# Rotary partners 64 partitions apart, two exchange transfers a half tile; gate and memory stores issued by ScalarE

## The chip, the core and the metric

The kernel runs on one core of a Trainium2 chip. The metric is the device time of one execution in microseconds (us). Five engines work in parallel, each through its own list in a fixed order: PE (matmul, with its weight loads shown as PEld), DVE (VectorE), ACT (ScalarE), POOL (GpSimd) and SP (SyncE, which here only issues transfers). 16 DMA engines carry the transfers. They synchronise through semaphores, so an instruction that waits holds everything behind it on its own engine.

## The reference

One layer of a hybrid encoder over 1024 tokens of width 1024: a mixer (windowed attention beside a gated delta rule), cross-attention into 256 memory tokens, a feed-forward block. What the change touches is the rotary embedding of attention queries and keys, the gate of the delta rule's output, and the memory's keys and values:

```python
def _rope(x, positions):                      # x: (b, s, heads, 64)
    half = x.shape[-1] // 2
    ...
    x1, x2 = xf[..., :half], xf[..., half:]
    return jnp.concatenate([x1 * cos - x2 * sin, x2 * cos + x1 * sin], axis=-1)
...
proj = h @ w_in[l]
aq, ak, av, dqkv, dgate, dalpha, dbeta = jnp.split(proj, IN_SPLITS, axis=-1)
aq = _rope(aq.reshape(b, s, ATTN_HEADS, ATTN_HEAD_DIM), positions)
ak = _rope(ak.reshape(b, s, ATTN_KV_HEADS, ATTN_HEAD_DIM), positions)
...
o = o * jax.nn.silu(gate.astype(jnp.float32).reshape(b, s, DN_HEADS, DN_HEAD_V))
...
kv = mem_n @ w_kv
k = kv[..., :D_MODEL].reshape(b, m, CROSS_HEADS, CROSS_HEAD_DIM)
v = kv[..., D_MODEL:].reshape(b, m, CROSS_HEADS, CROSS_HEAD_DIM)
```

Within a head of 64 values, value i and value i + 32 are rotary partners: each of the two outputs needs both.

## The kernel before

**Layout.** Activations of the mixer lie turned: features on the 128 partitions, tokens along the free axis in two halves of 512. Matmuls of float32 data run in three passes: each operand is split into a rounded part and a rest (`split`, L100: an ACT cast, then a DVE or POOL subtraction, L103 and L104), and hi x hi, lo x hi and hi x lo are summed in PSUM (`gemm_b`, L257). `load_w` (L118) fetches a weight tile of 128 input rows x 8 x 128 columns and splits it; `proj` (L265) multiplies it with the turned input, giving two PSUM tiles of 128 features x 512 tokens.

**Stages.** First the input is normalised and the delta rule's q, k, v are projected, convolved and turned into products (`ORDER_1`). Second come, in the order of `ORDER_2`, the attention projections (A: `attn_proj`, four tiles of queries and one of keys, tile 4), the attention values (V), the gates (G: `gate_proj`, four tiles), the last levels of the delta rule's block inverses (L: `levels`, which loads blocks of the base inverse, `d_inv`, and stores its result to `d_pz`), and the first attention windows (W). Third comes the scan over eight chunks in both directions for two groups of heads (`scan`, loads of `kv` and `pz`), and between its steps the other windows and the memory's keys (K) and values (V) (`ORDER_3`). Then follow output projection, cross-attention and feed-forward, from L1053 on.

**Rotary.** In `attn_proj` (L750) a half tile of 128 features (two heads of 64) x 512 tokens is multiplied by the sines into `sn` (L757) and by the cosines into `rop` (L758). Partners are 32 partitions apart, so the sine product has to change partitions: four transfers from SBUF to SBUF, each of 32 partitions, copy `sn` into `rot` with neighbouring groups of 32 exchanged (L760 to L762). The sum (L763) is stored as 128 rows of 512 values to `d_q` or `d_k` in DRAM (L764). The sign of the sine comes from a constant column (L72). `sn` and `rot` are two halves of one tile with two buffers; `rop` has two buffers, which it shares with the gate tile `gt`. Windows load queries back from `d_q` (`qr`, L644) and keys from `d_k` (`kraw`, L700), with the features of a head in their natural order.

**Stores.** Every transfer of the program is issued by SP, in one list: the gate stores (L784), the stores of memory keys (L953) and of memory values (L971) too. The gate store waits for the Silu of ACT (L783), the other two for the ACT copy out of PSUM (L952, L970). `d_gate` is read in the second half of the scan, `d_mk` and `d_mv` before cross-attention (L1127).

**Order.** The program is written as above, but a scheduler that works from a timeline model sets the order of each engine's list when it is built; weight loads have a higher priority (`AHEAD`). An edit in one place therefore moves instructions nearby.

Of the kernel before, what the change touches and what calls it, by code (L numbers as in the profile page):

```python
# [19 lines left out]
P = 128  # L20
S = 1024
D = 1024
KT = D // P
NT = S // P
HALF = 512
# [18 lines left out]
_ROPE_AT = len(_NAMES) * P  # L44
# [3 lines left out]
def host_constants():  # L48
    i = np.arange(P)
    blk = i // 32  # L50
    a, b = i[:, None], i[None, :]
    ba, bb = blk[:, None], blk[None, :]
    tri = {
        "ident": a == b,
        "mU": a < b,
        "mL": a > b,
        "mUi": a <= b,
        "mLi": a >= b,
        "m5": (ba // 2 == bb // 2) & (ba != bb),
        "m6": ba // 2 != bb // 2,  # L60
        "ones": a + b >= 0,
    }
    out = np.zeros((P, _NCONST), np.float32)
    for n, m in tri.items():
        out[:, _AT[n]:_AT[n] + P] = m

    out[:, _AT["band0"]:_AT["band0"] + P] = np.where(b >= a, 0.0, NEG)
    out[:, _AT["band2"]:_AT["band2"] + P] = np.where(b <= a, 0.0, NEG)
    half = np.arange(32, dtype=np.float32)
    inv = np.power(np.float32(10000.0), -half / np.float32(32)).astype(np.float32)  # L70
    out[:, _ROPE_AT] = inv[i % 32]
    out[:, _ROPE_AT + 1] = np.where(i % 64 < 32, 1.0, -1.0)  # L72
    return out


# [1 line left out]
def tile_hybrid_block(  # L77
# [4 lines left out]
    g_ffn_pre, w_gate_up, w_down, g_ffn_post, consts, out, dump=None, stop=None,  # L82
):
    nc = tc.nc
    x, mem, out = x[0], mem[0], out[0]
    w_in, w_out, w_cq, w_ckv, w_co = w_in[0], w_out[0], w_cq[0], w_ckv[0], w_co[0]
# [7 lines left out]
    def f32(ap):  # L94
        return ap.bitcast(F32)
# [4 lines left out]
    def split(hi, lo, src, scale=None, eng=None):  # L100

        if scale is None:
            nc.scalar.copy(hi, src)  # L103
            return (eng or nc.vector).tensor_tensor(lo, src, f32(hi), ALU.subtract)  # L104
        nc.scalar.activation(hi, src, AF.Identity, scale=scale)
        return nc.vector.scalar_tensor_tensor(lo, src, scale, f32(hi), ALU.mult, ALU.subtract)

    def pool(name, bufs, **kw):
        return tc.tile_pool(name=name, bufs=bufs, reuse_waits="tile", **kw)
# [5 lines left out]
    dram = ctx.enter_context(tc.tile_pool(name="dram", bufs=1, space=DRAM))  # L115
    wp = ctx.enter_context(pool("wp", 2))

    def load_w(src, k, n, eng=None, after=None, place=None):  # L118

        with tc.high_priority(AHEAD):  # L120
            raw = place or wp.tile([P, k, n], F32, tag="wraw", name="wraw")
            with ExitStack() as order_:
                if after:
                    order_.enter_context(tc.issue_after(after.ins))
                nc.sync.dma_start(raw, src.rearrange("(k p) n -> p k n", p=P))
            hi = wp.tile([P, k, n], F32R, tag="whi", name="whi")
            lo = wp.tile([P, k, n], F32R, tag="wlo", name="wlo")
            split(hi, lo, raw, eng=eng)
        return hi, lo


# [44 lines left out]
    d_q = dram.tile([512, S], F32, name="d_q")  # L176
    d_k = dram.tile([P, S], F32, name="d_k")
    d_gate = dram.tile([512, S], F32, name="d_gate")
# [7 lines left out]
    d_mk = dram.tile([D, ML], F32, name="d_mk")  # L186
    d_mv = dram.tile([2, P, D], F32, name="d_mv")
# [24 lines left out]
    for hf in range(2):  # L212
        hi = hx.tile([P, KT, HALF], F32R, name=f"hhi{hf}")
        lo = hx.tile([P, KT, HALF], F32R, name=f"hlo{hf}")
        for j in range(4):
            t = 4 * hf + j
# [9 lines left out]
            for kq in range(2):  # L226
# [4 lines left out]
                o = slice(4 * kq, 4 * kq + 4), slice(j * P, (j + 1) * P)  # L231
# [25 lines left out]
    def gemm_b(whi, wlo, act, psums, nk=KT):  # L257

        for ah, p_ in zip(act, psums):
            for k in range(nk):  # L260
                for i, (w, a) in enumerate(((whi, 0), (whi, 1), (wlo, 0))):
                    nc.tensor.matmul(p_, w[:, k, :], ah[a][:, k, :], start=(k == 0 and i == 0),  # L262
                                     stop=(k == nk - 1 and i == 2))

    def proj(src_cols, eng=None):  # L265
        whi, wlo = load_w(src_cols, KT, P, eng)
        pp = [pg.tile([P, 512], F32, tag="pg", name="pg") for _ in range(2)]
        gemm_b(whi, wlo, hT, pp)
        return pp
# [23 lines left out]


    ws = [load_w(dcols(1, h), KT, P, after=xload[t]) for h, t in ((0, 1), (1, 3))]
    pps = [[None, None], [None, None]]
    for hf in range(2):
# [14 lines left out]
    for hf in range(2):  # L312
        pp = pg.tile([P, 512], F32, tag="pg", name="pg")
# [67 lines left out]
    for hf in range(2):  # L381
        sl = slice(hf * HALF, (hf + 1) * HALF)
# [363 lines left out]
    def pair():  # L746
        t = ra.tile([P, 2, HALF], F32, tag="rr", name="rr", bufs=2)
        return t[:, 0], t[:, 1]

    def attn_proj(ct):  # L750
        pp = proj(w_in[:, ct * P:(ct + 1) * P])
        dst = d_q[ct * P:(ct + 1) * P, :] if ct < 4 else d_k
        for hf in range(2):
            sl = slice(hf * HALF, (hf + 1) * HALF)
            rop = trp.tile([P, HALF], F32, tag="rop", name="rop")
            sn, rot = pair()
            nc.vector.tensor_tensor(sn, pp[hf], sinT[:, sl], ALU.mult)  # L757
            nc.vector.tensor_tensor(rop, pp[hf], cosT[:, sl], ALU.mult)  # L758

            for q in range(4):  # L760
                o = 32 * (q ^ 1)
                nc.sync.dma_start(rot[32 * q:32 * q + 32], sn[o:o + 32])  # L762
            nc.vector.tensor_tensor(rop, rop, rot, ALU.add)  # L763
            nc.sync.dma_start(dst[:, sl], rop)  # L764

    def value_proj():

# [10 lines left out]
    def gate_proj(h):  # L778

        pp = proj(w_in[:, 2304 + h * P:2304 + (h + 1) * P])  # L780
        for hf in range(2):
            gt = trp.tile([P, HALF], F32, tag="rop", name="gt")
            nc.scalar.activation(gt, pp[hf], AF.Silu)  # L783
            nc.sync.dma_start(d_gate[h * P:(h + 1) * P, hf * HALF:(hf + 1) * HALF], gt)  # L784

    issue(ORDER_2, {"A": attn_proj, "V": value_proj, "G": gate_proj, "L": levels, "W": next_windows})
    dump("d_q", d_q); dump("d_k", d_k); dump("d_gate", d_gate)
    p1.close()
# [153 lines left out]
    def next_keys():  # L942

        ct = kv_done[0]
        kv_done[0] += 1
        whi, wlo = load_w(w_ckv[:, ct * P:(ct + 1) * P], KT, P, nc.gpsimd)
        pp = pc.tile([P, 512], F32, tag="pc", name="pck")[:, 0:ML]
        for k in range(KT):
            for i, (w, a) in enumerate(((whi, 0), (whi, 1), (wlo, 0))):
                nc.tensor.matmul(pp, w[:, k, :], mT[a][:, k, :], start=(k == 0 and i == 0), stop=(k == KT - 1 and i == 2))  # L950
        cv = mk.tile([P, 512], F32, tag="cv", name="cv", bufs=2)[:, 0:ML]
        nc.scalar.copy(cv, pp)  # L952
        nc.sync.dma_start(d_mk[ct * P:(ct + 1) * P, :], cv)  # L953

    def next_values():

        ch = kv_done[1]
        kv_done[1] += 1
        pp = [pc.tile([P, 512], F32, tag="pc", name="pcv") for _ in range(2)]
        for kp in range(4):  # L960
            whi, wlo = load_w(w_ckv[kp * 256:(kp + 1) * 256, D + ch * 512:D + (ch + 1) * 512], 2, 512)
            for t in range(2):
                for kk in range(2):
                    k = 2 * kp + kk
                    for i, (w, a) in enumerate(((whi, 0), (whi, 1), (wlo, 0))):
                        nc.tensor.matmul(pp[t], mT[a][:, k, t * P:(t + 1) * P], w[:, kk, :], start=(k == 0 and i == 0),
                                         stop=(k == KT - 1 and i == 2))
        for t in range(2):
            vv = mk.tile([P, 512], F32, tag="cv", name="vv", bufs=2)
            nc.scalar.copy(vv, pp[t])  # L970
            nc.sync.dma_start(d_mv[t, :, ch * 512:(ch + 1) * 512], vv)  # L971

    scans = [scan(g) for g in range(2)]

    def scan_step(pairs):

        for _ in range(4):
            for s_ in pairs:
                next(s_, None)

    issue(ORDER_3, {"s": lambda *gs: scan_step([scans[g] for g in gs]), "W": next_windows, "M": memory_norm,
                    "K": next_keys, "V": next_values})
    dump("d_pz", d_pz[0] + d_pz[1])
    dump("d_kv", d_kv)
# [124 lines left out]
    for hf in range(2):  # L1109
        for kp in range(4):  # L1110
            k2 = slice(2 * kp, 2 * kp + 2)
            raw = raws[hf]
# [22 lines left out]
    raw = LR2.enter_context(pool("raw2", 1, side="right")).tile([P, KT, HALF], F32, name="oraw")  # L1135
# [362 lines left out]
    for e in range(EARLY):  # L1498
        f = 2 * e
        w, A = [], []  # L1500
        for i, c0 in enumerate((f * P, FF + f * P)):
            place = fw.tile([P, KT, P], F32, tag=f"fw{i}", name="wraw") if e == EARLY - 1 else None
            whi, wlo = first_gate[i] if e == 0 else load_w(w_gate_up[:, c0:c0 + P], KT, P, place=place)
# [270 lines left out]
    for t in range(4):  # L1774
# [13 lines left out]
        r = 4 + t  # L1788
# [41 lines left out]
```

## Time and profile before

| | us |
|---|---|
| median of 3 runs | 1531.19 |
| lowest and highest run | 1529.92, 1532.13 |
| the profiled execution | 1531.03 |
| its span, first to last instruction | 1529.3 |
| ScalarE (ACT) busy | 752.0 |
| GpSimd (POOL) busy | 364.1 |
| granted TensorE clock, mean share of full | 0.994 |
| first exchange transfer issued, last | 208.7, 326.2 |
| first gate store issued, last | 268.2, 365.1 |
| first store of memory keys issued, last of memory values | 394.9, 557.4 |

Times in the profile count from the start of the span. A line such as L764 is the line of the kernel printed above. SPq, PEq and the like are an engine's issuing of instructions; "x4" counts instructions; "<-" behind an idle time names what ended it. A transfer has two times: the issue on its engine, and its landing, when its data has arrived and its semaphore is complete.

### The profile page before, as it was taken

To read this page: it belongs to the slowest core of one execution; us is meant where nothing else is said; L and a number is where in the kernel's file an instruction comes from. 1 tells how busy PE (TensorE), PEld (TensorE's weight loads), DVE (VectorE), ACT (ScalarE), POOL (GpSimd) and SP (SyncE) were. 2 spreads that over 40 slices of the span, in tenths; PEclk is the share of its full clock that TensorE was granted. 3 is DMA by queue.
4 is the path that set the end of the run, shared out by engine and by line. 5 is a ranking of instruction groups with operands and counts; after the bars stand their busy time and mean duration, and the time that the engine had idled before them with its cause. 6 is when DMAs were issued, how large, how long until landed. Compare 5 with 4: busy or idle time off the path is not lost.

```text
span 1529.3 us, 21202 instructions
## 1 busy us (share of the span) xinstructions
PE 1475.7 (96%) x7403; PEld 1239.1 (81%) x7403; DVE 1116.3 (73%) x1805; ACT 752.0 (49%) x1541; POOL 364.1 (24%) x369
## 2 busy tenths in 40 slices
PE   6999999998999999999999999999999999999997
PEld 5888888877889778888788877888888888888786
DVE  6868999787888866538567768676867774696665
ACT  5578821447557764455544685223222332454532
POOL 2020221311226203252201002433534342000021
PEclk9999999999999999999999999999999999999999
DMA  6235575856987584458725554343434333853355
GB/s 208 76 109 148 144 194 142 218 176 173 322 279 236 186 296 152 141 167 271 241 97 173 192 182 134 97 138 116 146 109 153 124 103 111 321 208 97 104 177 167
DMA packets 275159, 261.06 MB, mean 171 GB/s; under 512 B 34904, under 2 KB 206829, under 8 KB 275053
## 3 DMA queue, kind: packets, MB, share of 16 engines
q1 hardware_dynamic: 275053, 259.71, 53.9%
q8 instruction: 58, 0.95, 0.3%
q14 instruction: 48, 0.39, 0.1%
HBM read 181.25 MB, written 75.79 MB: 168 GB/s over the span
## 4 chain that ended last, share of the span: by engine, by line
PE 61%; DVE 10%; DMA 10%; ACT 4%; issue 3%; SPq 2%; POOL 1%; DVEq 0%; POOLq 0%; ACTq 0%
PE pD L1481 7%; PE pE L1481 7%; PE pA L1481 6%; PE pmg L1071 6%; PE pdX L1687 6%; PE pst L1287 5%; PE pcq L262 4%; PE pB L1481 3%; PE psc L810 2%; PE pdA L1687 2%; PE pdD L1687 2%; PE pg L262 2%; DMA wraw<-in_w_gate_up_dram 1%; PE pco L1186 1%; PE pdX L1784 1%
## 5 line engine op out<-in xcount | busy, mean ns | idle before, releaser
L103 ACT CAST whi<-wraw 128x1024 fp32r<-128x1024 f32 x96 | 100.8, 1051 | 133.0 <-DMA wraw<-in_w_gate_up_dram 37.0
L262 PE MATMUL pg<-hlo,whi 128*128 128x512 f32 x352 | 139.1, 396 | 0.0
L262 PE MATMUL pg<-hhi,whi 128*128 128x512 f32 x352 | 139.1, 396 | 0.0
L262 PE MATMUL pg<-hhi,wlo 128*128 128x512 f32 x352 | 138.1, 393 | 0.0
L104 POOL TENSOR_TENSOR wlo<-wraw,whi 128x1024 fp32r<-128x1024 f32 x36 | 88.3, 2453 | 189.6 <-ACT whi L103 188.2
L1481 PE MATMUL pA<-b,whi 128*128 128x512 f32 x352 | 111.9, 400 | 3.6 <-ACT m L1508 2.8
L104 DVE TENSOR_TENSOR wlo<-wraw,whi 128x1024 fp32r<-128x1024 f32 x60 | 76.0, 1269 | 46.0 <-ACT whi L103 42.4
L1481 PEld LDWEIGHTS pA<-b,whi 128*128 128x128 f32 x352 | 66.5, 192 | 19.2 <-ACT m L1508 4.0
L1687 PE MATMUL pdX<-dhl,whi 128*128 128x512 f32 x264 | 76.1, 390 | 1.5 <-ACT dhl L103 0.8
L262 PEld LDWEIGHTS pg<-hhi,whi 128*128 128x128 f32 x352 | 66.3, 189 | 13.4 <-ACT hhi L103 0.2
L262 PEld LDWEIGHTS pg<-hhi,wlo 128*128 128x128 f32 x352 | 66.2, 188 | 12.8
L262 PEld LDWEIGHTS pg<-hlo,whi 128*128 128x128 f32 x352 | 66.2, 188 | 12.7
L1564 POOL TENSOR_TENSOR act<-act,up 128x512 f32<-128x512 f32 x33 | 50.7, 1538 | 83.1 <-DVE up L1563 61.8
L1481 PE MATMUL pA<-b,wlo 128*128 128x512 f32 x176 | 69.9, 398 | 0.5 <-DVE wlo L104 0.5
L103 ACT CAST whi<-araw 128x1024 fp32r<-128x1024 f32 (+1 forms) x36 | 35.3, 982 | 67.9 <-PE pdX L1687 27.6
L104 DVE TENSOR_TENSOR wlo<-araw,whi 128x1024 fp32r<-128x1024 f32 (+1 forms) x36 | 40.9, 1135 | 36.1 <-ACT whi L103 35.7
L1536 POOL TENSOR_TENSOR sr<-wraw 128x512 f32<-128x512 f32 x22 | 30.3, 1379 | 150.7 <-DMA wraw<-in_w_gate_up_dram 98.7
L287 DVE SCALAR_TENSOR_TENSOR acc<-cp,cols,acc 128x1024 f32<-128x1024 f32 x48 | 62.1, 1297 | 0.1
L1687 PEld LDWEIGHTS pdX<-dhl,whi 128*128 128x128 f32 x264 | 49.3, 188 | 12.7 <-ACT dhl L103 1.1
L1721 POOL TENSOR_SCALAR frs<-sq 128x1 f32<-128x1 f32 x8 | 11.9, 1497 | 194.5 <-ACT jk L1706 193.6
L103 ACT CAST dhl<-b 128x512 fp32r<-128x512 f32 x66 | 40.3, 620 | 31.6 <-PE pdA L1687 13.7
L1481 PE MATMUL pB<-s0h,s1h 128*128 128x512 f32 x176 | 54.5, 391 | 0.0
(484 smaller groups left out, 4285.5 us busy)
## 6 DMA issues: line engine op xcount, KB each, us to landing
wraw<-in_w_gate_up_dram SPq DMA_DIRECT2D x54, 512.0 KB, 3.9
kv<-d_kv SPq DMA_DIRECT2D x32, 512.0 KB, 7.5
wraw<-in_w_in_dram SPq DMA_DIRECT2D x22, 512.0 KB, 4.2
b<-in_w_down_dram SPq DMA_DIRECT2D x20, 512.0 KB, 8.0
araw<-d_as SPq DMA_DIRECT2D x20, 512.0 KB, 3.7
pz<-d_pz SPq DMA_DIRECT2D x32, 256.0 KB, 7.6
wraw<-in_w_ckv_dram SPq DMA_DIRECT2D x16, 512.0 KB, 6.3
wraw<-in_w_out_dram SPq DMA_DIRECT2D x16, 512.0 KB, 3.7
```

The source lines that it names most:

```text
L103: nc.scalar.copy(hi, src)
L104: return (eng or nc.vector).tensor_tensor(lo, src, f32(hi), ALU.subtract)
L262: nc.tensor.matmul(p_, w[:, k, :], ah[a][:, k, :], start=(k == 0 and i == 0), stop=(k == nk - 1 and i == 2))
L287: nc.vector.scalar_tensor_tensor(acc, cp[:, t:t + S], taps[t], acc, ALU.mult, ALU.add)
L810: nc.tensor.matmul(out[:, d, h, :], lt[:, d, h, :], rt[:, d, h, :], start=True, stop=True)
L1071: nc.tensor.matmul(pp[t], act[a][:, k, tt], w_[:, kk, :], start=(k == 0 and i == 0), stop=(k == KT - 1 and i == 2))
L1186: nc.tensor.matmul(po, vr_[a][:, kt, cs], pts[kt][b_], start=(kt == 0 and i == 0), stop=(kt == 1 and i == 2))
L1287: nc.tensor.matmul(bank, a[:, tt], w, start=(start and i == 0), stop=(stop and i == 2), skip_group_check=not check)
L1481: nc.tensor.matmul(out_, w[a][:, k, :], xx[b_][:, k, :], start=(start and k == 0 and i == 0), stop=(k == HK - 1 and i == 2), skip_group_ch ...
L1536: nc.gpsimd.tensor_tensor(s[0], b_[:, 0:HK], b_[:, HK:], ALU.add)
L1564: nc.gpsimd.tensor_tensor(o_, o_, up, ALU.mult)
L1687: nc.tensor.matmul(banks[t], a[:, k - k0, tt], w, start=(first and k == 0 and i == 0), stop=(k == NB - 1 and i == 2), skip_group_check=not ...
```

## The change

The weight columns of the five attention tiles are put in another order as they are split: `load_w` gets `turned_pairs`, and with it casts and subtracts in two parts, so that the first halves (32 features) of both heads stand in columns 0 to 63 and the second halves in columns 64 to 127. After the matmul, partners are then 64 partitions apart. The exchange takes two transfers of 64 partitions. The sign column changes with the layout. The store takes the features back to their natural order in DRAM, in two transfers of 64 partitions, whose destination is 2 heads x 32 features x 512 tokens. Apart from that, the stores of gates, memory keys and memory values are issued by ScalarE.

```diff
-    out[:, _ROPE_AT + 1] = np.where(i % 64 < 32, 1.0, -1.0)
+    out[:, _ROPE_AT + 1] = np.where(i < 64, 1.0, -1.0)
...
-    def load_w(src, k, n, eng=None, after=None, place=None):
+    def load_w(src, k, n, eng=None, after=None, place=None, turned_pairs=False):
...
-            split(hi, lo, raw, eng=eng)
+            if turned_pairs:
+                for a in range(2):
+                    to = [t[:, :, 64 * a:64 * a + 64].rearrange("p k (h r) -> p k h r", h=2) for t in (hi, lo)]
+                    split(*to, raw.rearrange("p k (h a r) -> p k h a r", h=2, a=2)[:, :, :, a], eng=eng)
+            else:
+                split(hi, lo, raw, eng=eng)
...
-    def proj(src_cols, eng=None):
-        whi, wlo = load_w(src_cols, KT, P, eng)
+    def proj(src_cols, eng=None, **kw):
+        whi, wlo = load_w(src_cols, KT, P, eng, **kw)
...
-        pp = proj(w_in[:, ct * P:(ct + 1) * P])
-        dst = d_q[ct * P:(ct + 1) * P, :] if ct < 4 else d_k
+        pp = proj(w_in[:, ct * P:(ct + 1) * P], turned_pairs=True)
+        dst = (d_q[ct * P:(ct + 1) * P, :] if ct < 4 else d_k).rearrange("(h a r) t -> a h r t", h=2, a=2)
...
-            for q in range(4):
-                o = 32 * (q ^ 1)
-                nc.sync.dma_start(rot[32 * q:32 * q + 32], sn[o:o + 32])
+            for a in range(2):
+                nc.sync.dma_start(rot[64 * a:64 * a + 64], sn[64 - 64 * a:128 - 64 * a])
             nc.vector.tensor_tensor(rop, rop, rot, ALU.add)
-            nc.sync.dma_start(dst[:, sl], rop)
+            for a in range(2):
+                nc.sync.dma_start(dst[a, :, :, sl], rop[64 * a:64 * a + 64])
...
-            nc.sync.dma_start(d_gate[h * P:(h + 1) * P, hf * HALF:(hf + 1) * HALF], gt)
+            nc.scalar.dma_start(d_gate[h * P:(h + 1) * P, hf * HALF:(hf + 1) * HALF], gt)
...
-        nc.sync.dma_start(d_mk[ct * P:(ct + 1) * P, :], cv)
+        nc.scalar.dma_start(d_mk[ct * P:(ct + 1) * P, :], cv)
...
-            nc.sync.dma_start(d_mv[t, :, ch * 512:(ch + 1) * 512], vv)
+            nc.scalar.dma_start(d_mv[t, :, ch * 512:(ch + 1) * 512], vv)
```

## The prediction, made before the result was known

> **What bounds the kernel now.** I read the page first, then the busy time by stage, then the chain of waits in the stage that the change touches.
>
> ```profile
> span 1529.3 us, 21202 instructions
> PE 1475.7 (96%) x7403; PEld 1239.1 (81%) x7403; DVE 1116.3 (73%) x1805; ACT 752.0 (49%) x1541; POOL 364.1 (24%) x369
> ...
> 190.00:340.00 150.00, 145.16 (x783) 122.42 (x781) 128.25 (x252) 51.03 (x124) 34.97 (x53) 1.00 0.71 188
> 340.00:380.00 40.00, 36.28 (x231) 31.66 (x229) 30.27 (x78) 29.13 (x65) 5.30 (x9) 1.00 0.55 151
> 380.00:560.00 180.00, 168.69 (x1172) 152.97 (x1173) 146.28 (x362) 114.49 (x291) 60.14 (x70) 0.97 0.83 261
> 560.00:880.00 320.00, 317.57 (x1563) 266.10 (x1561) 202.41 (x297) 169.56 (x331) 69.81 (x54) 1.00 0.55 184
> ```
>
> Columns of the stage rows: length, then PE, weight load, DVE, ACT and POOL busy (instructions), granted clock, share of the DMA engines, GB/s. The ten rotary half tiles lie between 207 and 333 us, the gate stores between 268 and 366, the memory key and value stores between 394 and 558. So the change lives in 190 to 560. PE is idle there for 370 - (145.16 + 36.28 + 168.69) = 19.9 us: that is about all that better order or earlier transfers can give (busy PE includes pipelining, so a little more may hide in it). From 560 on PE is idle 2.4 us in 320 and nothing is edited.
>
> The granted clock is full, so matmul work is fixed and the question is what its inputs wait for. The chain of waits over 185 to 380 us names it:
>
> ```profile
> by line: PE pg L262 10.3%; DMA d_pz<-Z 8.9%; DMA kv<-d_kv 6.0%; issue 5.7%; DMA rr<-rr 5.0%; DVE acc L287 4.8%; SPq L762 3.8%; DMA qr<-d_q 3.5%; DVE D L588 2.9%; SPq L565 2.0%; DMA d_inv<-A 2.0%; DVE wlo L104 1.9%; PE ps L604 1.8%; PE ps L6
> ...
> 216.91 3.08 DMA cz<-d_inv
> ...
> 226.86 4.09 DMA rr<-rr
> ...
> 331.07 7.06 DMA d_pz<-Z
> ...
> 371.87 11.68 DMA kv<-d_kv
> ```
>
> Many short links, and the largest that are not PE are landings of transfers: stores of the level matrices, the exchange, loads of the scan. PE runs in a fixed order, so a late landing stops it even where projection matmuls stand behind. A change that makes transfers land later is therefore paid, one that frees issue time gains little.
>
> **The change part by part.** The sum is made against the profiled execution, 1531.03 us (its span 1529.3 plus 1.7 around it); the median of the runs is 1531.19.
>
> *Exchange, 40 transfers to 20.*
>
> ```profile
> 237.82 2.42 SPq L762 DMA_DIRECT2D rr<-rr  x4
> 244.22 0.33 SPq L764 DMA_DIRECT2D d_q<-rop  x1
> ...
> 248.54 1.12 SPq L700 DMA_DIRECT2D kraw<-d_k  x2
> ```
>
> Four issues of 32 partitions hold SP 2.42 us; two of 64 partitions, the shape of the key loads, 1.12. That is 1.3 us a half tile, 13 over ten. The chain has SPq L762 at 3.8% of 195 us, 7.4 us; 1.12/2.42 of that remains, so at most 4.0 goes. Lower bound of the gain 0, as the last landing may be hidden anyway. PE has 4.8 us idle in 190 to 340 to give; I take half the upper bound: -2.
>
> *The stores of the rotated tiles, 10 to 20.* The transfer of 128 rows becomes two, whose destination is written 2 x 32 x 512: the leading dimension counts 2, where it counted 128. On SP it is 2 x 0.56 for 0.33, +0.8 a half tile after the add, which only takes back part of the 13 us. What matters is how many of the 16 DMA engines carry it. No transfer here has a leading dimension of 2. The nearest rows are five narrow loads at the start; the answer for the first 30 us lists 24 issues, all landed:
>
> ```profile
> DMA packets 6445, 7.59 MB, mean 253 GB/s; under 512 B 728, under 2 KB 5165, under 8 KB 6445
> ...
> rows<-in_conv_w_dram SPq DMA_DIRECT2D x1, 30.0 KB, 7.7
> rows<-in_g_cross_pre_dram SPq DMA_DIRECT2D x1, 4.0 KB
> rows<-in_g_mem_dram SPq DMA_DIRECT2D x1, 4.0 KB
> rows<-in_g_ffn_pre_dram SPq DMA_DIRECT2D x1, 4.0 KB
> rows<-in_g_dn_out_dram SPq DMA_DIRECT2D x1, 0.5 KB
> prm<-in_a_log_dram SPq DMA_DIRECT2D x1, 4.0 KB, 5.6
> ```
>
> Of the 728 small packets, 3 x 128 are the 32-byte rows of the three prm loads. 344 remain, marks of completion. 24 transfers with 16 each would leave 384; 40 are missing, and loads of 60, 8, 8, 8 and 1 rows leave 40 if they run on 15, 8, 8, 8 and 1 engines (1 + 8 + 8 + 8 + 15). So a transfer runs on as many engines as divide its leading dimension. The price comes from one store seen alone, 244.2 to 246.3 us:
>
> ```profile
> DMA packets 144, 0.26 MB, mean 125 GB/s; under 512 B 16, under 2 KB 16, under 8 KB 144
> ...
> q1 hardware_dynamic: 144, 0.26, 33.0%
> ```
>
> 33.0% of 16 engines over 2.1 us are 11.1 engine-us. On 16 engines that is 0.69 us each, on two 5.54. Lower bound of the extra: 0 (spread as now). Upper: 4.85 us a half tile on two engines, 48.5 over ten. I take the upper, since the narrow loads are nearer in shape than any 128-row store. The Trainium skill's "DMA: Bandwidth & Descriptors", section "Why a DMA increments its semaphore by 16 and not by 1", says the engine count is the largest number up to 16 that divides the slowest dimension of both sides; the 40 missing marks agree, by it this store gets two engines, and with sixteen the sum below would be 8 us lower.
>
> What is late then:
>
> ```profile
> 209.00:332.00 123.00, 119.22 (x648) 100.89 (x647) 103.22 (x215) 41.88 (x106) 32.57 (x51) 1.00 0.70 181
> ...
> L588 DVE TENSOR_TENSOR Z<-cz,dmask 128x512 f32<-128x512 f32 x16 | 11.3, 724 | 7.3 <-DMA d_pz<-Z 7.0 <-DMA cz<-d_inv 0.3
> ```
>
> Those engines are busy 0.70 x 123 = 86.1 us already; with 48.5 they need 134.6 in 123, so they end 11.6 us behind. Every 128-row transfer has a share on them and lands when the last does: the other exchange half, cz and Ul for the levels, d_pz stores (DVE already waits 7.0 us for their landing before it can rewrite Z), qr, and the first kv and pz loads. The built order puts eight such stores of A0 and A1 within two tiles, straight ahead of the level stores and the stores of the second base inverse. PE's idle 123 - 119.2 = 3.8 us absorbs part: 11.6 - 3.8 = 7.8. Bounds of the exposure 0 and, with each of cz, rr and kv late by one pair besides, 11.6 + 5.5 = 17. I take +8.
>
> *Gate and memory stores issued by ACT.*
>
> ```profile
> SPq L691 <- DVE ao L690: 12.8, 4, 3.9
> ...
> SPq L784 <- ACT z L615: 10.8, 1, 10.8
> ...
> SPq L953 <- ACT cv L952: 4.3, 2, 3.7
> ...
> L784 SPq DMA_DIRECT2D d_gate<-gt x8: 326/382/932, 268.2 to 365.1; - x8
> ...
> L953 SPq DMA_DIRECT2D d_mk<-cv x8: 320/332/811, 394.9 to 515.9; - x8
> ```
>
> SP loses a wait of 10.8 us between 336 and 348, but next behind it stands the store of ao, which has its own wait, then a d_pz store that needs the level result; the scan's loads of kv need what the last projection frees. So the relief is worth little: bounds 0 and -4 (the PE idle of 340 to 380 is 3.7), taken -1. ACT gets 20 issues of 0.33 to 0.38 us, 7 us. Behind each wait the next casts and exponentials. ACT is busy 194.7 of 370 us, which covers it at 0; uncovered it is +7. The Trainium skill, same page, section "Issuing engines are not separate DMA queues", says transfers from several engines share the same 16 and only issue time is saved; no run here shows the second queue, and by it this part stays at -1.
>
> *Split in halves.* A 128x1024 cast becomes two of 128x512, and the subtraction likewise.
>
> ```profile
> L103 ACT CAST whi<-wraw x18: 1031/1048/1057, 378.3 to 555.9; 128x1024 fp32r<-128x1024 f32 x18
> ...
> L646 ACT CAST qs<-qr x16: 617/620/643, 284.1 to 506.7; 128x512 fp32r<-128x512 f32 x16
> ...
> L757 DVE TENSOR_TENSOR rr<-pg,sct x10: 677/686/692, 207.9 to 322.2; 128x512 f32<-128x512 f32 x10
> ...
> L104 DVE TENSOR_TENSOR wlo<-wraw,whi x10: 1214/1224/1765, 499.4 to 557.0; 128x1024 fp32r<-128x1024 f32 x10
> ```
>
> ACT: 2 x 0.62 - 1.05 = 0.19, DVE: 2 x 0.69 - 1.22 = 0.16, five tiles each: 1.0 and 0.8. Both sit ahead of a projection, DVE is busy 128 of 150 us: bounds 0 and 2, taken +1.
>
> *Order.* The built program moves more than the edit: DVE issues the casts and rotary steps of A0's halves together, PE runs the two halves of a level's block side by side instead of staggered. The same matmuls, and the first scan product and the last projection stand at the same place in PE's work. Bounds -10 and +10 (half the 19.9 us of idle either way), taken 0.
>
> Sum: 1531.0 - 2 + 8 - 1 + 0 + 1 + 0 = **1537 us**.
>
> **The rivals.**
>
> *The relief of SP rules, faster.* If the stores are hidden, or spread, the exchange gives its 4.0, the gate wait its 4, and the new order part of its 10: 1531 - 8 = 1523. For it: SPq L762 is in the chain; the store is the last step of its tile, and its readers (kraw, qr) come much later. Against: the 40 missing marks.
>
> *Nothing to be seen.* Late landings eat what SP frees: 1531 within 0.2% (3 us, about what a measurement of this kernel can tell from no change). Both terms are small against 1531, but they would have to match.
>
> *ACT holds the scan.* Where transfers back up, a store's issue can hold its engine as long as SP's longest gate store, 0.93 us, instead of 0.33; between 380 and 560 ACT is busy 64% and PE waits for its casts. 20 x 0.9 = 18 us, half exposed, on top of the stores: 1537 + 9 = 1546. It decides as soon as ACT's issues average over 0.6 us.
>
> *It doesn't do what it says.* A rotary tile's issues fall from 10 to 8 only, since the stores double. If the exchange is not on the path either, what is left is +8 + 1: 1540, inside the forecast.
>
> **How the numbers follow.** Slower by the stores, around 1537: 0.55. ACT besides, around 1546: 0.12. No difference: 0.07. Faster, around 1523: 0.26. The forecast's own range is 1533 to 1548 (exposure 4 to 17 us beside small terms of a few). The faster case holds more than 2 in 10, so the range must reach it: 1522 to 1556, the top from 17 for the stores and half the loss of order or ACT. Faster by over 0.2%: 0.26, within: 0.08, slower: 0.66.
>
> **What would show it.** Stores: d_q<-rop and d_k<-rop of 128 KB landing in over 4 us (2.0 now), the kv, cz and rr landings longer, DVE's wait before Z over 7.0. If they land in 2, the term of +8 falls and the faster case is left. Exchange: 20 issues of about 0.56 us, SPq L762's successor near half of its 3.8% of the chain. Gates: no SP wait for L784 or L953, ACT's issues near 0.35. PE's idle between 190 and 380 should grow from 8.6 to some 15 us, the first output projection matmul start after 556 us, and all behind it keep its length. An earlier start of it would prove me wrong.

## The result, and the profile after

| | before | after |
|---|---|---|
| median, us | 1530.67 (5 runs, 1528.84 to 1532.13) | 1571.31 (5 runs, 1566.61 to 1573.84) |
| ratio, 95% interval | | 1.0265, 1.0245 to 1.0284 |
| span of the profiled execution, us | 1529.3 | 1568.4 |
| first scan product, first output projection matmul, us | 365.7, 555.6 | 398.1, 594.6 |

The change makes the kernel 40.6 us slower. The direction was forecast, the size was not: 1537 was said, with 1556 as the upper end.

The head of the page of after, with what the DMA queues moved:

```profile
span 1568.4 us, 21197 instructions
PE 1488.2 (95%) x7403; PEld 1252.3 (80%) x7403; DVE 1113.8 (71%) x1810; ACT 753.5 (48%) x1546; POOL 360.6 (23%) x369
...
DMA packets 274719, 261.05 MB, mean 166 GB/s; under 512 B 34464, under 2 KB 206389, under 8 KB 274613
```

The span grew by 39.1 us. PE's busy time grew by 12.5 for the same 7403 matmuls (1475.7 before), so 26.6 us are idle time of PE and 12.5 us are matmuls that took longer (the last section shows how). The packets under 512 B confirm the engine count of the stores. Before had 34904 of them:

```profile
DMA packets 275159, 261.06 MB, mean 171 GB/s; under 512 B 34904, under 2 KB 206829, under 8 KB 275053
```

By the prediction's reading each engine that carries a transfer leaves one small packet, its mark of completion. Twenty transfers fewer in the exchange take away 20 x 16 = 320 marks. Ten stores with 16 marks each are 160, twenty with 2 each are 40, which takes away 120. Together that is 440, and 34904 - 34464 = 440.

Busy time by stage, columns as in the prediction:

```profile
190.00:340.00 150.00, 134.05 (x674) 113.82 (x673) 110.11 (x219) 42.53 (x107) 30.86 (x51) 0.92 0.63 157
340.00:380.00 40.00, 34.59 (x166) 29.05 (x165) 24.25 (x58) 15.27 (x35) 1.49 (x2) 0.83 0.40 124
380.00:560.00 180.00, 162.27 (x1198) 152.30 (x1197) 141.82 (x374) 113.39 (x304) 64.89 (x77) 0.97 0.77 232
```

In 190 to 340 PE is busy 11.1 us less than before although its matmuls are slower (granted clock 0.92, it was 1.00), and the DMA engines are less busy too: 0.63 where they were 0.71. The same rows on fewer engines did not fill the engines. They left them emptier.

What DVE waits for names the place. This is the tile of the exchange in after: its issues on SP (ns shortest, median, longest), then the idle time that ended with its landing (us in total, times). Below it are the same wait and the landing times (us) in before:

```profile
L766 SPq DMA_DIRECT2D rr<-rr x20: 462/584/2234, 207.6 to 346.7; - x20
...
  DMA rr<-rr: 26.2, 7
```

```profile
  DMA rr<-rr: 1.8, 1
...
DMA to landing us min/median/max: 1.9/2.0/5.8
```

And this is the chain of waits of after over 185 to 420 us, with four of its steps (start and length in us, then what):

```profile
by line: DMA rr<-rr 17.6%; PE pg L267 10.1%; DMA pz<-d_pz 7.8%; DMA d_pz<-Z 7.6%; issue 4.1%; DVE acc L292 3.8%; DMA wraw<-in_w_ckv_dram 3.6%; PE ps L609 3.4%; DVE A L552 3.2%; DVE tmpb L550 3.1%; DVE Z L593 2.7%; DVE rr L762 2.4%; SPq L766
...
257.26 0.61 DVE rr L762
257.89 0.51 SPq L766
258.44 6.78 DMA rr<-rr
265.31 0.69 DVE rop L767
```

The exchange's landings are 17.6% of 235 us, 41 us of the chain; before they were 5.0% of 195, some 10 us. One of them took 6.78 us: the product is ready at 257.9, SP issues at once, and the add starts at 265.3. Two short stretches show what the DMA engines do meanwhile:

```profile
252.00:254.00 2.00, 2.00 (x10) 1.68 (x9) 1.96 (x5) 0.00 (x0) 0.48 (x2) 1.00 0.13 42
...
263.00:264.00 1.00, 1.00 (x10) 0.92 (x8) 0.00 (x0) 0.00 (x0) 0.00 (x0) 1.00 0.13 51
```

A share of 0.13 is 2 of 16 engines. Two engines work off the stores issued at 249.5 to 252.1 and what stands behind them, so fourteen of sixteen are idle on average, and the exchange, which has rows on all sixteen, can't land before these two have reached its rows. DVE's timeline shows the next one, and what it makes late:

```profile
276.01 0.69 DVE L767 TENSOR_TENSOR rop<-rop,rr 128x512 f32<-128x512 f32 x1 [4.52 <-DMA rr<-rr]
...
277.46 0.43 DVE L632 TENSOR_SCALAR Z<-ps 64x256 f32<-64x256 f32 x1
```

DVE stands 4.52 us at an add whose result is needed much later, and a level result, `Z`, which PE needs at once, is behind it in DVE's list. (In this wait the other engines are not idle to the end: a weight load that SP issued at 271.1, behind the exchange, brings the share to 0.76 and more from 272 to 275.)

### The profile page after: what moved, and what is told of

Its sections match the earlier page's. It is cut to its first block, busy times and chain, and to the rows that moved or that the text cites. A ratio compares the mean times of both kernels' runs of the same rounds, so it can differ in the third digit from the quotient of the medians.

```text
span 1568.4 us, 21197 instructions
## 1 busy us (share of the span) xinstructions
PE 1488.2 (95%) x7403; PEld 1252.3 (80%) x7403; DVE 1113.8 (71%) x1810; ACT 753.5 (48%) x1546; POOL 360.6 (23%) x369
## 2 busy tenths in 40 slices
DMA packets 274719, 261.05 MB, mean 166 GB/s; under 512 B 34464, under 2 KB 206389, under 8 KB 274613
## 4 chain that ended last, share of the span: by engine, by line
PE 65%; DVE 12%; DMA 11%; ACT 5%; issue 3%; POOL 1%; SPq 1%; ACTq 0%; DVEq 0%; POOLq 0%
PE pD L1486 7%; PE pE L1486 7%; PE pg L267 7%; PE pA L1486 6%; PE pmg L1076 6%; PE pdX L1692 6%; PE pst L1292 5%; PE pdA L1692 4%; PE pcq L267 3%; PE pB L1486 3%; DMA rr<-rr 3%; PE psc L815 2%; PE pdD L1692 2%; PE pdX L1789 1%; DMA wpart<-in_w_co_dram 1%
## 5 line engine op out<-in xcount | busy, mean ns | idle before, releaser
L103 ACT CAST whi<-wraw 128x1024 fp32r<-128x1024 f32 (+1 forms) x101 | 101.3, 1008 | 161.8 <-PE pg L267 39.5
L267 PE MATMUL pg<-hhi,wlo 128*128 128x512 f32 x352 | 141.3, 402 | 0.0
L104 DVE TENSOR_TENSOR wlo<-wraw,whi 128x1024 fp32r<-128x1024 f32 (+1 forms) x65 | 75.1, 1160 | 49.3 <-ACT whi L103 46.7
```

## The experiments

Each ratio is to the runs of before that were made beside it (their medians lie between 1529.1 and 1531.6). "Wide" stores run on 16 engines, "narrow" ones on 2.

| kernel | median, us | ratio | 95% interval |
|---|---|---|---|
| after (narrow, 20 stores on ACT) | 1571.3 | 1.0265 | 1.0245 to 1.0284 |
| after, those 20 stores back on SP | 1559.2 | 1.0206 | 1.0181 to 1.0231 |
| after, stores wide | 1539.8 | 1.0070 | 1.0049 to 1.0090 |
| after, stores wide and those 20 back on SP | 1530.4 | 1.0004 | 0.9994 to 1.0015 |
| after, stores wide, gate alone on ACT | 1534.0 | 1.0020 | 1.0006 to 1.0035 |
| before, 20 stores on ACT | 1539.7 | 1.0063 | 1.0042 to 1.0085 |
| before, gate stores alone on ACT | 1527.6 | 0.9992 | 0.9982 to 1.0002 |
| before, memory stores alone on ACT | 1540.3 | 1.0073 | 1.0059 to 1.0088 |
| before, memory stores on GpSimd | 1532.6 | 1.0016 | 1.0003 to 1.0029 |
| before, store written 2 x 64 x 512 (still wide) | 1529.6 | 1.0004 | 0.9988 to 1.0020 |
| before, narrow by padding | 1555.7 | 1.0176 | 1.0160 to 1.0191 |
| the same, issued by ACT | 1554.9 | 1.0165 | 1.0144 to 1.0186 |
| before, wide, issued by ACT | 1531.8 | 1.0013 | 1.0000 to 1.0026 |
| before, 4 early of 10 narrow | 1539.3 | 1.0052 | 1.0034 to 1.0070 |
| before, 4 late of 10 narrow | 1540.9 | 1.0061 | 1.0038 to 1.0083 |

### Which part of the change it is

*After, with the stores of gates and memory on SP.*

```diff
-            nc.scalar.dma_start(d_gate[h * P:(h + 1) * P, hf * HALF:(hf + 1) * HALF], gt)
+            nc.sync.dma_start(d_gate[h * P:(h + 1) * P, hf * HALF:(hf + 1) * HALF], gt)
...
-        nc.scalar.dma_start(d_mk[ct * P:(ct + 1) * P, :], cv)
+        nc.sync.dma_start(d_mk[ct * P:(ct + 1) * P, :], cv)
...
-            nc.scalar.dma_start(d_mv[t, :, ch * 512:(ch + 1) * 512], vv)
+            nc.sync.dma_start(d_mv[t, :, ch * 512:(ch + 1) * 512], vv)
```

> After, with the 20 stores of gates and of memory keys and values issued by SP again; the rotary part stays. Theory A (the stores of the rotated tiles carry the loss): 1560 to 1578. Theory C (ACT's issues carry it): 1530 to 1550. My recorded term for SP's relief (-1): 1 us slower than after, about 1572.

It measured 1559.2, just under the range of theory A: most of the loss stays, 12 us go. DVE still waits 24.1 us for the exchange.

*Before, with these 20 stores on ACT* (the opposite edit on the other kernel):

> Before, with the 20 stores of gates and of memory keys and values issued by ACT; the rotary part is that of before. Theory A: 1525 to 1536, no wait of SP for the gate store. Theory C: over 1540, ACT's issues over 0.6 us each. My recorded terms (0 for ACT, -1 for SP): about 1530.

1539.7. That is 10 us, not the 0 of the prediction. But ACT's issues took 0.326 us each (the median for gates, memory keys and memory values alike), not over 0.6. So nearly the effect that theory C gives is there (over 1540), and the sign by which it was to be known is not.

*After, with wide stores.* Interleaving the two heads in the turned columns makes 32 features the leading dimension of the store, without moving one instruction:

```diff
-    out[:, _ROPE_AT] = inv[i % 32]
+    out[:, _ROPE_AT] = inv[i % 64 // 2]
...
-                    to = [t[:, :, 64 * a:64 * a + 64].rearrange("p k (h r) -> p k h r", h=2) for t in (hi, lo)]
+                    to = [t[:, :, 64 * a:64 * a + 64].rearrange("p k (r h) -> p k h r", h=2) for t in (hi, lo)]
...
-        dst = (d_q[ct * P:(ct + 1) * P, :] if ct < 4 else d_k).rearrange("(h a r) t -> a h r t", h=2, a=2)
+        dst = (d_q[ct * P:(ct + 1) * P, :] if ct < 4 else d_k).rearrange("(h a r) t -> a r h t", h=2, a=2)
```

> After, with the two heads interleaved in the turned columns (partition 64a + 2r + h), so that the destination of each store is 32 x 2 x 512 where it was 2 x 32 x 512; the order of instructions on every engine is that of after, the casts of the ten halves read and write with a stride. Theory A: 14 marks more for each of 20 stores, 34464 to 34744 packets under 512 B; DVE's wait for the exchange falls from 26.2 us to under 5, the time to 1522 to 1535. Theory B (the order): it stays at 1560 to 1572. Theory C (the issues of ACT): it stays at 1560 to 1572 too. The strided casts should add under 2 us.

Its queues, and the tile of its exchange:

```profile
DMA packets 275000, 261.05 MB, mean 170 GB/s; under 512 B 34745, under 2 KB 206670, under 8 KB 274894
```

```profile
  DMA rr<-rr: 3.8, 5
...
DMA to landing us min/median/max: 2.2/2.3/2.9
```

281 small packets more than after (280 were expected). The exchange lands in 2.3 us, DVE waits 3.8 us for it in place of 26.2, and the time falls by 31.5 us to 1539.8. That is 5 us above the range given for theory A, which had left out the 10 us of ACT that this kernel still has.

*After, with both:* wide stores, and the 20 others on SP.

> After, with the heads interleaved (stores 32 x 2 x 512, sixteen engines) and the stores of gates and memory on SP: the rotary part alone, with its order, without narrow stores. If the loss of after is the narrow stores plus ACT's issues, and the order is worth nothing: 1526 to 1533. If the exchange's saving counts (my term -2, at most -4): 1525 to 1529. If the order of the halves costs: over 1535.

1530.4, a ratio of 1.0004: with wide stores on SP the rotary part changes nothing, faster or slower. Four corners result: 1.0004 with neither, 1.0206 with narrow stores, 1.0070 with ACT, 1.0265 with both. The two losses add up, within the interval of the last: 0.0206 + 0.0070 = 0.0276.

### Are the narrow stores enough by themselves

*Before, with the store written in two groups of rows.*

```diff
-            nc.sync.dma_start(dst[:, sl], rop)
+            nc.sync.dma_start(dst.rearrange("(g r) t -> g r t", g=2)[:, :, sl], rop)
```

> Before, with one edit: the destination of the store of a rotated tile is written 2 x 64 x 512 where it was 128 x 512; still one transfer, and the order of instructions on every engine is that of before. Theory A (the stores run on 2 of 16 DMA engines, and the exchange behind them in the queue waits): the store's 144 packets lose 14 marks each, 140 in all, so packets under 512 B go from 34904 to 34764; DVE's wait for the exchange grows from 1.8 us to over 10, and the time to 1550 to 1575. My recorded term (+8, the lateness paid once at the end): 1536 to 1548. Theory B (the new order of the halves is what costs, the stores are hidden): 1528 to 1535.

1529.6, and 34904 small packets, exactly as before. The edit reached nothing: the two groups of 64 rows adjoin, in the built program the destination is 128 x 512 again, and the transfer kept its sixteen engines. The run is a repeat of before and says nothing on theory A.

*Before, with a spare row after each head,* so that the groups don't adjoin:

```diff
-    d_q = dram.tile([512, S], F32, name="d_q")
-    d_k = dram.tile([P, S], F32, name="d_k")
+    d_q = dram.tile([8, 65, S], F32, name="d_q")
+    d_k = dram.tile([2, 65, S], F32, name="d_k")
...
-            nc.sync.dma_start(dst[:, sl], rop)
+            nc.sync.dma_start(dst[:, :, sl], rop)
```

(`dst` and the loads of queries and keys leave the spare rows out.)

> Before, with one spare row of DRAM after each head in the arrays of queries and keys, so that the one store of a rotated tile is 2 x 64 x 512 and can't be merged to 128 x 512; the order of instructions on every engine is that of before. If it runs on two engines, packets under 512 B fall by 140, to 34764. Theory A (two-engine stores hold what stands behind them in the queue, whatever the layout): DVE's wait for the exchange over 10 us, time 1550 to 1575. Theory D (they cost only with the halves of a tile side by side, as after has them, where two stores lie ahead of the next exchange): 1530 to 1545, wait under 6 us. My recorded term: 1536 to 1548.

Its queues, the tile of its exchange, and three lines of its waits between 185 and 420 us (engine, what waited, for what, us in total, times, longest):

```profile
DMA packets 275019, 261.05 MB, mean 168 GB/s; under 512 B 34764, under 2 KB 206689, under 8 KB 274913
```

```profile
DMA to landing us min/median/max: 3.7/5.2/6.7
```

```profile
POOL m L575 <- DMA cz<-d_inv: 17.9, 3, 9.3
...
DVE Z L588 <- DMA d_pz<-Z: 14.2, 6, 5.6
...
DVE rop L763 <- DMA rr<-rr: 10.0, 6, 3.4
```

34764, the 140 fewer that two engines give. With the instructions of before in the order of before, and nothing changed but the engine count and the addresses of the rows in DRAM, the kernel is 25.9 us slower, so theory D falls. The padding alone, with wide stores, was not run; but the kernel after, made wide without padding, gained 31.5 us. The exchange lands in 5.2 us, the median was 2.0. The wait for it is smaller than in after (10.0 against 26.2, just at the bound that theory A gave), but the waits for `d_pz` and `cz` grew, from 7.0 to 14.2 and from 10.3 to 17.9 us. Why the waits fall differently in the two orders is not shown.

### How a narrow store costs more than its engines are short of

*Whether the queue matters.* The same narrow stores in ACT's own queue, so that SP's queue holds nothing narrow, and as control the wide ones there:

```diff
-            nc.sync.dma_start(dst[:, :, sl], rop)
+            nc.scalar.dma_start(dst[:, :, sl], rop)
```

> Control of the next run: before, with its ten stores of rotated tiles (128 x 512, sixteen engines) issued by ACT, in ACT's own queue. Theory H: transfers land in 2 to 4 us in that stage, so ACT is held little: 1528 to 1540.

> The padded kernel (one store of 2 x 64 x 512 on two engines, SP's queue: 1555.7), with these ten stores issued by ACT, so that the exchange no longer stands behind them in SP's queue. Theory Q (the order within one queue makes the exchange and the other transfers wait): within 8 us of the control, DVE's wait for the exchange under 3 us where it was 10.0. Theory E (the two engines are busy 5.5 us whoever issues): 18 to 27 us over the control, the wait still near 10.

Control 1531.8, narrow 1554.9: 23 us apart. Two waits of the narrow run:

```profile
DVE Z L588 <- DMA d_pz<-Z: 15.9, 7, 5.8
...
DVE rop L763 <- DMA rr<-rr: 9.1, 6, 3.0
```

The wait for the exchange stays at 9.1 us (1.4 in the control). So theory Q falls: it is the two engines' time that is missing, whichever queue the stores stand in. The Trainium skill, "DMA: Bandwidth & Descriptors", section "Issuing engines are not separate DMA queues", says the same: the queues of the issuing engines run on one set of 16 DMA engines. These two runs agree.

*Whether it is the sum of the engines' work or each store by itself.* Four of the ten narrow, the early ones or the late ones; the arrays of the other queries aren't padded.

> The padded kernel with four of its ten stores on two engines, those of query tiles 0 and 1 (issued between about 244 and 279 us in it); the other six are 128 x 512 on sixteen engines; order of instructions as before. Packets under 512 B fall by 56, to 34848. Theory Sum (my recorded working: the two engines' extra work counts against what they have free, 123 - 86 = 37 us, and only the rest is late): 4 x 4.85 = 19 us extra, so nothing is late, 1527 to 1533. Theory Chain (each narrow store delays the exchange and the stores that follow it, which are a chain, and each delay is paid): 4/10 of the 23 to 27 us that ten cost, 1537 to 1543, with DVE's waits for the exchange and for d_pz together over 10 us in that stretch.

> The same with the stores of query tiles 2 and 3 (issued between about 321 and 353 us in the kernel with ten), the last before the scan, 34848 packets under 512 B. Theory Sum: 19 us extra against what is free there, 1527 to 1533. Theory Chain: 1537 to 1543, and this and the run with the first four add up to most of the 23 to 27 us of all ten.

1539.3 and 1540.9, 8 and 9 us over before. Both have 34848 small packets. By the prediction's count 19 us of extra work stand against 37 free ones, and they cost 8 us, so the sum is not what counts: each narrow store costs about 2 us, early or late. The eight make 17 of the 26 us that all ten cost; whether the other 9 are the two stores of keys or come from all being there together wasn't tried. DVE's waits, first with the early ones narrow, then with the late ones (before has 7.0 and 1.8):

```profile
DVE Z L588 <- DMA d_pz<-Z: 7.8, 5, 2.5
...
DVE rop L763 <- DMA rr<-rr: 6.5, 5, 3.1
```

```profile
DVE Z L588 <- DMA d_pz<-Z: 13.4, 7, 5.2
...
DVE rop L763 <- DMA rr<-rr: 4.5, 2, 4.1
```

With the early ones PE's busy time in 190 to 340 is 141.78 (145.16).

### What holds ACT

*Gate stores alone on ACT, and memory stores alone.*

> Before, with the eight gate stores alone issued by ACT. The whole of this part (20 stores) measured +10 us. Theory C1 (the scheduler's new order from the gate stores): 1535 to 1541. Theory C2 (the memory stores hold ACT in the scan): 1527 to 1533.

> Before, with the twelve stores of memory keys and values alone issued by ACT; the order on PE is that of before but for 12 lines. Theory C1: 1527 to 1533. Theory C2: 1535 to 1541, with PE's busy time of 380 to 560 us down by 4 or more from 168.7.

1527.6 and 1540.3: the twelve memory stores cost all of it, with PE's order unchanged but for 12 lines. Theory C2 holds, with the predicted fall of PE's busy time in 380 to 560 us (163.90, from 168.69). What ACT waited for between 376 and 575 us, and the first store in ACT's list:

```profile
ACT ph L103 <- DMA pz<-d_pz: 5.0, 1, 5.0
ACT vn L847 <- DMA pz<-d_pz: 4.7, 1, 4.7
...
ACT whi L103 <- DMA qr<-d_q: 3.7, 1, 3.7
```

```profile
391.95 0.35 ACT L952 COPY cv<-pck 128x256 f32<-128x256 f32 x1
392.20 0.58 ACT L103 CAST ph<-ptw 128x512 fp32r<-128x512 f32 x1
397.14 0.34 ACTq L953 DMA_DIRECT2D d_mk<-cv  x1
397.52 0.59 ACT L847 COPY vn<-psc 128x512 f32<-128x512 f32 x1 [4.74 <-DMA pz<-d_pz]
398.00 0.59 ACT L103 CAST ph<-ptw 128x512 fp32r<-128x512 f32 x1
```

The copy that the store needs is done at 392.3, yet the store is issued at 397.14, when a load of `pz` has landed. What holds it is an instruction of its own, a wait for a semaphore just ahead of each of the eight key stores:

```profile
L953 ACTq EVENT_SEMAPHORE  x8: 17/17/17, 397.1 to 522.4; - x8
```

The program as built from this kernel says what it waits for. Eight semaphores of transfers, DMAHW0 to DMAHW7, are shared in turn by all transfers that SP and ACT issue. A store is given one of them, and its issue waits until the earlier transfer that uses it has landed, besides waiting for its operand. For the first key store (DMAHW5) that is a load of `pz`, for the second a load of `qr`, for the third a load of `pz`: the three waits of ACT above, in the order 4.7, 3.7, 5.0.

On SP the same wait stood too (the same semaphore and the same load, at the same store), and held other transfers only. On ACT it holds the next cast of the scan, for which PE waits. This is PE at that moment:

```profile
398.65 0.50 PE L686 MATMUL pow<-ph,vhl 128*128 128x512 f32 x1 [3.10 <-ACT ph L103]
```

The three waits of ACT are 13.4 us. Before has no wait of ACT for `pz` in that stretch, and one of 4.8 us for a load of `qr`. PE stands 3.10 us behind the first hold and 2.52 behind the third; how the rest of the 10 us follows is not shown. In the run with the gate stores alone on ACT, between 263 and 366 us, none of the eight was issued more than 0.03 us after the instruction ahead of it had ended.

*Memory stores on GpSimd* tells the hold from its rival, that SP without these stores issues loads too early:

```diff
-        nc.sync.dma_start(d_mk[ct * P:(ct + 1) * P, :], cv)
+        nc.gpsimd.dma_start(d_mk[ct * P:(ct + 1) * P, :], cv)
...
-            nc.sync.dma_start(d_mv[t, :, ch * 512:(ch + 1) * 512], vv)
+            nc.gpsimd.dma_start(d_mv[t, :, ch * 512:(ch + 1) * 512], vv)
```

> Before, with the twelve stores of memory keys and values issued by GpSimd instead (SP: before; ACT: measured 1540). Theory H (a store's issue waits until an earlier scan load has landed, three such holds of 3.4 to 4.5 us on ACT, with the scan's copies behind them): GpSimd is 24% busy and has little behind the stores, so 1526 to 1534, and no wait of ACT for a pz load. Theory S (SP, without these waits, issues loads earlier, which collide): SP's list is the same as with ACT, so 1536 to 1542.

1532.6, and no wait of ACT for `pz`. SP's list in the built program is the same as with ACT, and 8 us of the 10 are gone, so theory S falls: the hold is the cause. The run takes the hold away rather than moving it to an idle engine. In its built program GpSimd's transfers have semaphores of their own, and the eight key stores wait for their copy alone.

### Is there a faster version

> The change without what measured slow: heads interleaved (stores 32 x 2 x 512 on sixteen engines), two exchange transfers, gate stores on ACT, memory stores on SP. The parts measured 1.0004 and 0.9992 of before, so together 1525 to 1532; if SP's relief adds to the exchange's saving, under 1526.

1534.0 at 1.0020 (1.0006 to 1.0035), slightly slower than its parts let expect; why is open. Nothing tried beats before by more than a measurement can tell; gates alone on ACT (0.9992) come nearest.

## Why the prediction was right and wrong

**What bounds the kernel: right.** Late landings were paid, and everything from the first output projection matmul on keeps its length (973.7 us before, 973.8 after): the first scan product is 32.4 us later, that matmul 39.0, the end 39.1.

**Exchange, -2: not seen.** SP's side came as costed (0.584 us median for each of 20 issues, 0.56 forecast). But the rotary part with wide stores is at 1.0004 (0.9994 to 1.0015), so little or nothing is left of the gain. DVE waited only 1.8 us for the landing before, in ten half tiles. The halves (+1) and the order (0) are inside that same measurement; only the sum of the three is shown, near 0.

**The stores, +8: this is the step that failed.** The engine count, two, was right, by the missing marks and by the share of 0.13. So was the price, 5.5 us on each: in the packet records of after most rows of a store take 84 ns between 268.5 and 270.5 us, and 64 of them are 5.4 us. What failed is "What is late then": "those engines are busy 0.70 x 123 = 86.1 us already; with 48.5 they need 134.6 in 123, so they end 11.6 us behind". It treats the engines as if work were always there to fill their free time, and counts lateness once, at the end. But exchange, add and store are a chain, `Z`, `d_pz` and `cz` another, and all of them pass through DVE's one list and then PE's. While the two engines work off a store, what stands behind it waits, and while DVE waits little new is issued, so the free time is lost and not used: the share of the DMA engines fell to 0.63. The right count was by store: 4.85 us of extra engine time, of which 1.9 to 2.6 were paid in the order of before (7.7 us for four, 26 for ten), and 3.1 in after (1571.3 - 1539.8 = 31.5 us for ten half tiles). Why after pays more is not shown: only one tile's halves go together there (244.5 to 252.1 us), the others one at a time, as in before. The text even had the pieces: it said that every transfer with a share on these engines "lands when the last does", and that "the built order puts eight such stores of A0 and A1 within two tiles", and it set the upper bound at 17 by adding one late pair.

**A stall costs PE more than its length.** 12.5 of the 39.1 us are not idle time. The prediction had the clock as full and fixed; in after it fell to half in eleven stretches before the end of PE's work, 58.0 us in all, where before has four, 17.1 us in all. The last section shows one.

**SP's relief, -1: not contradicted.** Gates on ACT measured -2.1 us, which can't be told from 0 or from -1. The wait of 10.8 us for a gate was worth little, as argued.

**ACT, 0: wrong by 10.** "ACT is busy 194.7 of 370 us, which covers it" counts the issues (7 us) and misses what an issue waits for. The rival "ACT holds the scan" had the engine and the stage right, at 0.12, but its test was wrong: "it decides as soon as ACT's issues average over 0.6 us". They average 0.33; the hold stands before the issue, as a wait on an earlier transfer, and shows only as idle time of ACT.

**The sum, redone** with what was measured: 1531 + 31 (narrow stores, in the order of after) + 10 (memory stores on ACT) + 0 for the rest = 1572, against 1571.3. The 31 is itself a difference to after, so this shows that the parts add up and is no forecast; with the 26 us of the padded kernel it would be 1567.

**What would show it.** The exchange landing late, DVE's wait before `Z` over 7.0 us (9.3), rr x20 near 0.56 us, no SP wait for gates, a later first output projection matmul: all came. For the narrow stores themselves the trace of after gives no landing time. PE's idle in 190 to 380 was said to grow from 8.6 to 15 us; it is 190 - 134.05 - 34.59 = 21.4.

## What to carry to other kernels

When a transfer's written shape confines it to a few DMA engines, don't add its engine time to a budget of free time. Count it for each such transfer by itself, as lateness of whatever stands behind it in whichever queue and that an in-order engine waits for (here 1.9 to 3.1 us were paid each time, of 4.85). Or reorder the layout (here 32 x 2 for 2 x 32) so that the leading dimension spreads it, which measured 1.0004. Before a store is moved to a compute engine, look at everything that its issue waits for, not only its operand: a wait that goes unnoticed on an engine that only issues is paid where casts stand behind it.

## What was not expected of the hardware

The granted clock fell 2.1 us after PE's last matmul had ended, and came back 4.9 us after the next one began. In after PE waits from 270.55 to 277.94 for the level result of 277.46 that is shown above. The rows around it, by windows (columns as in the prediction) and by the timeline of PE (start and length in us):

```profile
270.00:271.00 1.00, 0.55 (x3) 0.13 (x1) 1.00 (x2) 0.00 (x0) 0.00 (x0) 1.00 0.31 72
...
272.00:273.00 1.00, 0.00 (x0) 0.00 (x0) 0.00 (x0) 0.00 (x0) 0.00 (x0) 0.81 0.76 180
273.00:274.00 1.00, 0.00 (x0) 0.00 (x0) 0.00 (x0) 0.00 (x0) 0.00 (x0) 0.50 1.07 276
...
282.00:283.00 1.00, 1.00 (x4) 0.78 (x3) 0.00 (x0) 0.00 (x0) 1.00 (x1) 0.56 0.76 210
```

```profile
270.16 0.39 PE L267 MATMUL pg<-hlo,whi 128*128 128x512 f32 x1
277.94 1.12 PE L600 MATMUL ps<-ident,Ul 128*128 128x128 f32 x4 [7.40 <-DVE Z L632]
...
281.42 0.63 PE L267 MATMUL pg<-hhi,whi 128*128 128x512 f32 x1
281.85 0.63 PE L267 MATMUL pg<-hlo,whi 128*128 128x512 f32 x1
...
283.72 0.39 PE L267 MATMUL pg<-hlo,whi 128*128 128x512 f32 x1
283.94 0.39 PE L267 MATMUL pg<-hhi,wlo 128*128 128x512 f32 x1
```

A mean of 0.81 in 272 to 273 puts the fall at 272.6, and 0.56 in 282 to 283 puts the return at 282.9. In between, matmuls of 128x512 follow each other every 0.43 us, where it is 0.23 at full clock. So a stall of 7.4 us is followed by some 5 us at half speed, and costs about 10, by an estimate from these rows. In the traces of before and after every stretch at half clock but the last lasts 3.4, 6.8 or 10.2 us. The Trainium skill, "TensorE: Matmul & The Clock Gate", "Part 1: The HAM clock gate", puts both turns at windows of about 3.4 us that run freely, the fall behind an idle one and the return behind a busy one. The return agrees: counted on from 272.6, the first window that lies wholly behind the first matmul is 279.4 to 282.9. The fall does not: PE was busy until 270.55 in the window that ended at 272.6, so 2.1 idle us were enough.

That a destination of 2 x 64 rows counts as 128 where the rows adjoin (34904 small packets), and as 2 with a spare row between (34764), was not expected either. The shape in the source text doesn't decide. What is left after adjoining rows are joined does, and they are joined when the program is built.
